# Later places in the queues for what follows the addition of a chunk's parts in the up projection (transformer layer, one Trainium2 core)

## The chip, the cores and the metric

The kernel runs on one core of one Trainium2 chip. The metric is the device time of one launch in microseconds (us): median of several runs.

## What is computed

One decoder layer for 256 tokens of width 2048: two kinds of attention, an output projection, and an MLP. Only the MLP matters here; in the reference it is

```python
h = _rmsnorm(x, norm_mlp_pre[layer])
u = jnp.square(jax.nn.relu(h @ w_up[layer]))
x = x + _rmsnorm(u @ w_down[layer], norm_mlp_post[layer])
```

`w_up` is 2048 x 8192 and `w_down` 8192 x 2048, all in float32.

## The kernel before

**Precision and units of work.** A float32 factor is split into a high and a low part (`split`, lines 303 to 307: ScalarE copies the source to `hi`, VectorE subtracts to get `lo`; `split_gain`, lines 309 to 312, does the same with a gain). A product is then three matmuls into one bank of PSUM, high by high, low by high, high by low; `three` issues such a group of three through `mm`, and every matmul of the MLP therefore has line 296. A transpose on TensorE is `transpose`, line 300.

**The up projection.** Its 8192 columns are done in eight chunks of 1024, numbered 0 to 7 (`for j in range(FF // CW)` in `layer`). A chunk has four accumulators of 128 tokens x 512 columns, one PSUM bank each: `PARTS` (0,0), (0,1), (1,0), (1,1), token block first, column half second. The steps of a chunk come from a table, `UP_STEPS`. A step `k` is one 128-row piece of the weights: four groups of three matmuls, one for each accumulator. A step `p` or `w` covers two pieces by a fast-multiplication scheme with seven products in place of eight (`seven_products`): its sums of weight blocks (`t`, `u`, made by VectorE from the raw blocks `ab`) are split like other weights, and four of its products go into four more banks, `m`. Chunks 1 to 5 have eight steps `k` and four of the other kind, chunks 6 and 7 ten and three. While chunk j runs, chunk j - 1's four banks are needed again for `m`, and their evacuation has to be over by then.

**Putting a chunk together.** The four `m` are combined after the last step of the seven-product kind (`close`, line 1072 on ScalarE, line 1075 on VectorE, result in tile `c`). At the end of the chunk's last step one generator `up_evac` is started for each accumulator. It adds the part from `c` to the accumulator in place (line 969, VectorE), applies Relu with the token's scale (line 973, ScalarE, tile `r`), transposes the four 128 x 128 blocks of `r` on TensorE back into the same bank (`rt`), and squares the bank into tile `uT` (line 991, ScalarE). `r` has two buffers. The tiles are numbered by column half: the halves of chunk 5 are `j` = 10 and 11 in `up_evac`, those of chunk 7 are 14 and 15. So `rt10_0` is chunk 5, first half, first token block.

**What sets the order.** Instructions are written in a fixed order, engine by engine. Besides the loop over matmuls there are generators; each yields the delay after which it wants to go on, and `Flow` keeps a model clock that only advances by the planned cost of TensorE's instructions (0.216 us for a matmul of 512 columns). After each group of three matmuls `flow.pump()` lets every generator whose time has come issue its next instructions. A delay therefore does not make any engine wait: it only decides behind which matmuls of the next chunk, and behind which splits of coming weights, an instruction stands in its engine's queue. In `up_evac` the delays are 0.2 us ahead of the addition, a fixed one behind it, then `UP_STEP` (2.2 us) times `order`, where `order` is 0.75 times the part's number 0 to 3, then the Relu, and `D_UP` (1.8 us) from there to the transposes, behind which the square follows directly. Since generators go on only after a group of three matmuls (0.65 us of the model clock), each delay is rounded up to whole groups.

Weights are split up to six tiles ahead of use into eight buffers `hi` and eight `lo`; a load into `raw` (five buffers, queue SP) or `ab` (queue POOL) is issued when its buffer is free.

After chunk 7 the down projection begins at once: its first matmuls (tile `y`) run while chunk 7 is put together, and its left factors are the `uT` tiles, split into `uhi` and `ulo`.

Of the kernel before, what the change touches and what calls it, by code (L numbers as in the profile page):

```python
# [263 lines left out]
def layer(nc, tc, io):  # L264
# [13 lines left out]
    def bank(i, name):  # L278
        return ps.tile([P, 512], F32, tag=f"bank{i}", bufs=1, name=name)
# [19 lines left out]
    def transpose(out, a):  # L299
        nc.tensor.transpose(out, a, ident)  # L300
        flow.spend(TR)
# [663 lines left out]
    def up_evac(j, b, i, acc, order, more=None):  # L965

        if more is not None:
            yield 0.2
            nc.vector.tensor_tensor(out=acc, in0=acc, in1=more, op=OP.add)
            yield 1.4  # L970
        yield UP_STEP * order
        r = late["up"].tile([P, 512], F32, tag="r", bufs=2, name=f"r{j}_{b}")
        nc.scalar.activation(r, acc, AF.Relu, scale=rstd2[b])
        yield D_UP if j > 1 else 2 * D_UP
        t = bank(i, f"rt{j}_{b}")
        for k in range(4):
            transpose(t[:, k * P:(k + 1) * P], r[:, k * P:(k + 1) * P])
        if j not in uT:
            if j in (12, 13):
                t2 = late["ab"][:, (j - 12) * CW:(j - 11) * CW]  # L980
            elif j in (8, 9):
                if j == 8:
                    late["uT8"] = late["up"].tile([P, 2 * CW], F32, tag="uT8", bufs=1, name="uT8")
                t2 = late["uT8"][:, (j - 8) * CW:(j - 7) * CW]
            elif j == 10:
                t2 = late["up"].tile([P, CW], F32, tag="uT10", bufs=1, name="uT10")
            else:
                tag = {"tag": "T", "bufs": 2} if j > 13 else {}
                t2 = late["up"].tile([P, CW], F32, name=f"uT{j}", **tag)
            uT[j] = t2.rearrange("p (k s) -> p k s", k=4)  # L990
        nc.scalar.activation(uT[j][:, :, b * P:(b + 1) * P], t.rearrange("p (k s) -> p k s", k=4), AF.Square)
# [91 lines left out]
    for j in range(FF // CW):  # L1083
# [9 lines left out]
        for t, b in order:  # L1093
# [18 lines left out]
            if what == "k":  # L1112
                w = weights.get(tiles[0])
                h_done(k, b)
                for n in range(2):
                    c = slice(n * 512, (n + 1) * 512)
                    three(accs[b, n], [tok(hT[x], k, b) for x in range(2)], [w[x][:, 0, c] for x in range(2)], t == 0, t == len(steps) - 1)
                    if t == len(steps) - 1:
                        evac.append(flow.start(up_evac(2 * j + n, b, at[b, n], accs[b, n], 0.75 * (2 * b + n),
                                                       more[b, n] if j else None)))  # L1120
                    flow.pump()
                if b == NB - 1:
                    weights.free(tiles[0])
                continue
# [208 lines left out]
```

## Time and profile before

| | |
|---|---|
| device time, median of 3 runs | 1051.41 us (1051.28 to 1051.68) |
| the profiled execution: its own time | 1050.67 us |
| the profiled execution: span from first to last instruction | 1048.9 us |
| TensorE matmul busy | 1036.4 us, 99% of the span |
| VectorE busy | 810.6 us, 77% |
| ScalarE busy | 633.0 us, 60% |
| mean granted TensorE clock | 0.998 |

The first line of the table is what a result is compared with. The profile is of one execution, whose span leaves out 1.77 us of its own time; positions below are microseconds from the span's start. PE is TensorE, PEld its weight loads, DVE VectorE, ACT ScalarE, POOL GpSimd and SP the queue that issues most loads. A row of the timeline has start, duration, engine, line, operation and tiles; in brackets stand the idle time of the engine before it and what ended that. Ends of matmuls are modelled, so starts are what is compared. The up projection's chunks 2 to 7 begin at about 444, 487, 530, 573, 616 and 660 us, and the down projection at 704 us.

### The profile page before, as it was taken

Reading aid. Unit: us, or ns where it says so; the run is one execution under the profiler, and the core shown is the slowest. Engines: PE = TensorE matmul, PEld = TensorE weight load, DVE = VectorE, ACT = ScalarE, POOL = GpSimd, SP = SyncE. Lnnn points to the kernel's source line nnn. Section 1 sums busy time; section 2 is a strip of 40 time slices with the busy share of each in tenths; the row PEclk is TensorE's granted clock in tenths of the full one; section 3 lists DMA queues with packets and bytes.
Section 4 is the critical chain, followed back from the end, with each engine's and each line's share of the span. In section 5 each row is a group of like instructions: output and inputs, shape, how many; then the busy total and the mean of one; then the engine's idle time right before and its main releaser. Section 6 shows DMA issues by size and latency. Waiting matters only on the chain.

```text
span 1048.9 us, 13584 instructions
## 1 busy us (share of the span) xinstructions
PE 1036.4 (99%) x4844; PEld 863.1 (82%) x4844; DVE 810.6 (77%) x1083; ACT 633.0 (60%) x846; POOL 98.9 (9%) x156
## 2 busy tenths in 40 slices
PE   9999999999999999999999999999999999999996
PEld 7888899888888788888888888888888888888885
DVE  6776546567557669988889798887899988989995
ACT  6675436565545466666756766656567564766661
POOL 0011111112111000010100000000000001112100
PEclk9999999999999999999999999999999999999999
DMA  9999879699878295766766656469778767788952
GB/s 298 369 298 298 221 197 321 197 258 300 227 219 259 84 362 180 281 207 241 262 214 222 228 191 212 139 227 322 249 272 312 267 226 260 264 301 318 368 196 81
DMA packets 93572, 260.81 MB, mean 249 GB/s; under 512 B 8768, under 2 KB 13376, under 8 KB 92096
## 3 DMA queue, kind: packets, MB, share of 16 engines
q1 hardware_dynamic: 71776, 190.61, 52.9%
q0 software_dynamic: 21152, 68.69, 23.0%
q8 instruction: 38, 0.62, 0.2%
q10 hardware_dynamic: 576, 0.64, 0.2%
q14 instruction: 30, 0.25, 0.1%
HBM read 244.18 MB, written 39.32 MB: 270 GB/s over the span
## 4 chain that ended last, share of the span: by engine, by line
PE 87%; DVE 6%; DMA 3%; issue 2%; ACT 2%; POOL 0%; DVEq 0%; POOLq 0%; SPq 0%; ACTq 0%
PE y L296 26%; PE acc_u L296 17%; PE acc_o L296 8%; PE m L296 6%; PE md L296 5%; PE acc_qk L296 4%; PE acc_v L296 4%; PE acc_cq L296 2%; PE acc_ukv L296 2%; PE acc_q L296 2%; PE acc_k L296 2%; DMA raw<-in_w_up 2%; DVE lo L307 2%; PE acc_uq L296 2%; PE acc_ckv L296 1%
## 5 line engine op out<-in xcount | busy, mean ns | idle before, releaser
L307 DVE TENSOR_TENSOR lo<-raw,hi 128x1024 fp32r<-128x1024 f32 (+3 forms) x241 | 269.7, 1137 | 96.3 <-ACT hi L306 95.5
L306 ACT ACTIVATE hi<-raw 128x1024 fp32r<-128x1024 f32 (+3 forms) x241 | 234.7, 988 | 98.0 <-PE y L296 21.5
L296 PE MATMUL y<-hi,uhi 128*128 128x512 f32 x376 | 146.7, 390 | 0.0
L296 PE MATMUL y<-hi,ulo 128*128 128x512 f32 x376 | 146.3, 389 | 0.0
L296 PE MATMUL y<-lo,uhi 128*128 128x512 f32 x376 | 146.3, 389 | 0.0
L296 PE MATMUL acc_u<-hi,hT_hi 128*128 128x512 f32 x356 | 141.7, 398 | 0.0
L296 PE MATMUL acc_u<-hi,hT_lo 128*128 128x512 f32 x356 | 139.2, 391 | 0.4 <-DVE hT_lo L307 0.4
L296 PE MATMUL acc_u<-lo,hT_hi 128*128 128x512 f32 x356 | 138.8, 390 | 0.0
L311 DVE SCALAR_TENSOR_TENSOR lo<-raw,gcol,hi 128x1024 fp32r<-128x1024 f32 x72 | 90.6, 1280 | 16.2 <-ACT hi L310 15.8
L310 ACT ACTIVATE hi<-raw,gcol 128x1024 fp32r<-128x1024 f32 x72 | 81.6, 1149 | 20.3 <-DMA raw<-in_w_up 12.8
L296 PEld LDWEIGHTS y<-hi,ulo 128*128 128x128 f32 x376 | 70.6, 188 | 14.8
L296 PEld LDWEIGHTS y<-hi,uhi 128*128 128x128 f32 x376 | 70.6, 188 | 14.6
L296 PEld LDWEIGHTS y<-lo,uhi 128*128 128x128 f32 x376 | 70.6, 188 | 14.4
L296 PEld LDWEIGHTS acc_u<-hi,hT_lo 128*128 128x128 f32 x356 | 66.8, 188 | 15.0 <-DVE hT_lo L307 0.8
L296 PEld LDWEIGHTS acc_u<-lo,hT_hi 128*128 128x128 f32 x356 | 67.0, 188 | 12.9
L296 PEld LDWEIGHTS acc_u<-hi,hT_hi 128*128 128x128 f32 x356 | 66.9, 188 | 12.9
L296 PE MATMUL m<-hi,st 128*128 128x512 f32 x156 | 56.5, 389 | 0.0
L296 PE MATMUL acc_o<-hi,mixT_hi 128*128 128x512 f32 x128 | 51.8, 405 | 0.0
L307 DVE TENSOR_TENSOR lo<-st_down,hi 128x1024 fp32r<-128x1024 f32 x40 | 48.0, 1220 | 3.9 <-ACT hi L306 3.8
L296 PE MATMUL acc_o<-hi,mixT_lo 128*128 128x512 f32 x128 | 50.2, 392 | 0.0
L296 PE MATMUL acc_o<-lo,mixT_hi 128*128 128x512 f32 x128 | 50.0, 390 | 0.0
L306 ACT ACTIVATE hi<-st_down 128x1024 fp32r<-128x1024 f32 x40 | 42.1, 1052 | 10.8 <-PE y L296 9.4
(331 smaller groups left out, 2037.6 us busy)
## 6 DMA issues: line engine op xcount, KB each, us to landing
raw<-in_w_down SPq DMA_DIRECT2D x88, 512.0 KB, 5.8
raw<-in_w_up SPq DMA_DIRECT2D x86, 512.0 KB, 4.6
raw<-in_w_in SPq DMA_DIRECT2D x55, 512.0 KB, 6.5
raw<-in_w_out SPq DMA_DIRECT2D x32, 512.0 KB, 7.3
ab<-in_w_up POOLq DMA_DIRECT2D x28, 512.0 KB, 5.1
sums<-in_w_up SPq DMA_DIRECT2D x20, 512.0 KB, 7.9
ab_down<-in_w_down POOLq DMA_DIRECT2D x20, 512.0 KB, 6.3
tu<-sums POOLq DMA_DIRECT2D x8, 1024.0 KB, 5.1
```

The source lines that it names most:

```text
L296: nc.tensor.matmul(out, a, b, start=start, stop=stop)
L306: nc.scalar.activation(hi, src, AF.Copy)
L307: nc.vector.tensor_tensor(out=lo, in0=src, in1=hi.bitcast(F32), op=OP.subtract)
L310: nc.scalar.activation(hi, src, AF.Copy, scale=g)
L311: nc.vector.scalar_tensor_tensor(out=lo, in0=src, scalar=g, in1=hi.bitcast(F32), op0=OP.mult, op1=OP.subtract)
```

## The change

One line: the delay that `up_evac` yields after the addition, where there is one (chunks 1 to 7). It was 1.4 us for all; now it is 1.8 us for column halves 2 to 9 (chunks 1 to 4) and 2.4 us for halves 10 to 15 (chunks 5, 6 and 7).

```diff
@@ -967,7 +967,7 @@
         if more is not None:
             yield 0.2
             nc.vector.tensor_tensor(out=acc, in0=acc, in1=more, op=OP.add)
-            yield 1.4
+            yield 1.8 if j < 10 else 2.4
         yield UP_STEP * order
         r = late["up"].tile([P, 512], F32, tag="r", bufs=2, name=f"r{j}_{b}")
         nc.scalar.activation(r, acc, AF.Relu, scale=rstd2[b])
```

No instruction is added or removed. On TensorE, the four transposes of each part of chunk 5 stand one group of three matmuls further on, here the first part's, in the second step of chunk 6 (`acc_u6` are chunk 6's accumulators, `hi258` and `lo258` a weight tile, `hT` the left factor):

```order
-L300 MATMUL rt10_0_5631<-ident_94,r10_0_5620 128x128 x4
 L296 MATMUL acc_u6_00_5608<-hi258_5527,hT_hi_2925 128x512
 L296 MATMUL acc_u6_00_5608<-lo258_5528,hT_hi_2925 128x512
 L296 MATMUL acc_u6_00_5608<-hi258_5527,hT_lo_2926 128x512
+L300 MATMUL rt10_0_5640<-ident_94,r10_0_5623 128x128 x4
```

The same holds for all four parts of chunks 5, 6 and 7; in chunks 1 to 4 only the last part, (1,1), moves, by one group as well, and nothing else does on any engine.

On ScalarE, at the same place (`r` Relu, `uT` square, `hi264` the split of a sum of weights that stands ahead of need):

```order
-L973 ACTIVATE r10_0_5620<-acc_u5_00_5233,rstd_pre20_3418 128x512
-L991 ACTIVATE uT10_5636<-rt10_0_5631 128x4x128
-L973 ACTIVATE r11_0_5638<-acc_u5_01_5234,rstd_pre20_3418 128x512
-L306 ACTIVATE hi264_5642<-u6_0_5550 128x1024
-L991 ACTIVATE uT11_5660<-rt11_0_5655 128x4x128
-L973 ACTIVATE r10_1_5662<-acc_u5_10_5235,rstd_pre21_3513 128x512
+L973 ACTIVATE r10_0_5623<-acc_u5_00_5233,rstd_pre20_3418 128x512
+L306 ACTIVATE hi264_5633<-u6_0_5550 128x1024
+L991 ACTIVATE uT10_5645<-rt10_0_5640 128x4x128
+L973 ACTIVATE r11_0_5647<-acc_u5_01_5234,rstd_pre20_3418 128x512
+L991 ACTIVATE uT11_5663<-rt11_0_5658 128x4x128
+L973 ACTIVATE r10_1_5665<-acc_u5_10_5235,rstd_pre21_3513 128x512
```

The first Relu keeps its place; the split `hi264` now stands ahead of the first square and the second Relu, not behind them. Chunk 6's parts in chunk 7 move in the same way.

On ScalarE at the start of the down projection, where chunk 7 is put together (`uhi0_1` and `hi308` are splits of a left factor and of a weight tile):

```order
-L973 ACTIVATE r14_0_6359<-acc_u7_00_5971,rstd_pre20_3418 128x512
-L991 ACTIVATE uT14_6375<-rt14_0_6370 128x4x128
-L973 ACTIVATE r15_0_6377<-acc_u7_01_5972,rstd_pre20_3418 128x512
-L306 ACTIVATE uhi0_1_6379<-uT1_3816 128x1024
-L306 ACTIVATE hi308_6385<-raw308_6383 128x1024
+L973 ACTIVATE r14_0_6362<-acc_u7_00_5971,rstd_pre20_3418 128x512
+L306 ACTIVATE uhi0_1_6370<-uT1_3816 128x1024
+L306 ACTIVATE hi308_6376<-raw308_6374 128x1024
+L991 ACTIVATE uT14_6388<-rt14_0_6383 128x4x128
+L973 ACTIVATE r15_0_6390<-acc_u7_01_5972,rstd_pre20_3418 128x512
```

Here two splits pass the first square and the second Relu. On VectorE the splits' second halves (`lo264` and its like) keep their places; POOL's queue is the same, and so is SP's.

## The prediction

> **What bounds the kernel now.** I read the page's first lines, then the view of waits for TensorE, then the timeline at each place where the change moves something.
>
> ```profile
> span 1048.9 us, 13584 instructions
> PE 1036.4 (99%) x4844; PEld 863.1 (82%) x4844; DVE 810.6 (77%) x1083; ACT 633.0 (60%) x846; POOL 98.9 (9%) x156
> ...
> PE rt L300 <- ACT r L973: 1.2, 3, 0.5
> ```
>
> TensorE is busy 1036.4 of 1048.9 us. Only 12.5 us are left, head and tail of the program among them, so what a new order can gain is small, and what it can lose is whatever new wait it gives TensorE. The third line is what the change can touch: the transposes of a chunk's Relu tile waited for that Relu three times, 1.2 us in all, at most 0.5 us at a time. The timeline shows where. First TensorE where chunk 5 is put together; the second piece is the next transposes there, which wait for nothing:
>
> ```profile
> 618.07 0.39 PE L296 MATMUL acc_u<-hi,hT_lo 128*128 128x512 f32 x1
> 618.98 0.65 PE L300 MATMUL rt<-ident,r 128*128 128x128 f32 x4 [0.52 <-ACT r L973]
> 619.39 0.49 PE L296 MATMUL acc_u<-hi,hT_hi 128*128 128x512 f32 x1
> 619.72 0.40 PE L296 MATMUL acc_u<-lo,hT_hi 128*128 128x512 f32 x1
> ...
> 621.34 0.40 PE L296 MATMUL acc_u<-hi,hT_lo 128*128 128x512 f32 x1
> 621.58 0.60 PE L300 MATMUL rt<-ident,r 128*128 128x128 f32 x4
> 621.93 0.48 PE L296 MATMUL acc_u<-hi,hT_hi 128*128 128x512 f32 x1
> 622.24 0.39 PE L296 MATMUL acc_u<-lo,hT_hi 128*128 128x512 f32 x1
> ```
>
> From the last matmul ahead of the transposes to the second one behind them pass 619.72 - 618.07 = 1.65 us with the wait and 622.24 - 621.34 = 0.90 us without. The stall costs 0.75 us, more than the 0.52 that the bracket counts, because the modelled ends of matmuls hide some of it and the restart is a little slower. The same where chunk 6 is put together, and the remaining places: chunk 1 (first line) and chunk 7 (last three lines).
>
> ```profile
> 447.39 0.66 PE L300 MATMUL rt<-ident,r 128*128 128x128 f32 x4 [0.17 <-ACT r L973]
> ...
> 662.21 0.39 PE L296 MATMUL acc_u<-hi,hT_lo 128*128 128x512 f32 x1
> 663.12 0.66 PE L300 MATMUL rt<-ident,r 128*128 128x128 f32 x4 [0.52 <-ACT r L973]
> ...
> 663.84 0.39 PE L296 MATMUL acc_u<-lo,hT_hi 128*128 128x512 f32 x1
> ...
> 706.33 0.39 PE L296 MATMUL y<-hi,ulo 128*128 128x512 f32 x1
> 706.56 0.60 PE L300 MATMUL rt<-ident,r 128*128 128x128 f32 x4
> 709.08 0.38 PE L300 MATMUL rt<-ident,r 128*128 128x128 f32 x2
> ```
>
> For chunk 6 the stall is 663.84 - 662.21 - 0.90 = 0.73 us. Chunk 7's transposes begin 0.23 us after the matmul ahead of them, the ordinary step: no wait there. Chunk 1's wait of 0.17 us is at its first part, which the change doesn't move.
>
> **The change, part by part.** *The first transposes of chunks 5 and 6* go behind one more group of three matmuls. One group lasts 0.68 us on TensorE (first line, from the chain); the other lines are the Relu that is waited for at 618.98 with the addition ahead of it, and the Relu at 663.12.
>
> ```profile
> 632.00 0.68 PE m L296 x3
> ...
> 617.51 1.89 DVE L969 TENSOR_TENSOR acc_u<-acc_u,c 128x512 f32<-128x512 f32 x3
> ...
> 618.24 0.69 ACT L973 ACTIVATE r<-acc_u,rstd_pre 128x512 f32<-128x512 f32 x1 [4.12 <-DVE acc_u L969]
> ...
> 662.38 0.69 ACT L973 ACTIVATE r<-acc_u,rstd_pre 128x512 f32<-128x512 f32 x1 [4.12 <-DVE acc_u L969]
> ```
>
> ScalarE had been idle 4.12 us before this Relu: it starts when VectorE's addition ends, wherever it is queued, and its place behind `hi263` is the old one. So it still ends at 618.24 + 0.69 = 618.93. TensorE, without waiting, would now come to the transposes at 618.07 + 0.23 + 0.68 = 618.98, the very time at which they began with the wait, 0.05 after the Relu's end. For chunk 6: Relu over at 663.07, TensorE there at 662.21 + 0.23 + 0.68 = 663.12, where they began too. The wait is filled with a group of useful matmuls and nothing is left of it, but with no margin.
>
> The gain at each place is therefore at least the group that is now done ahead, 0.68 us, and at most the whole stall, 0.75 and 0.73. Two places give 1.36 to 1.48 us. The difference is the slower restart, 0.05 to 0.07 a time, which stays if `r` comes only just in time. I take 1.4, nearer the lower end, since 0.05 us is no lead.
>
> [...]
>
> *Whether the second gain adds to the first* depends on VectorE. If VectorE's additions for chunk 6 came at a fixed time, TensorE, 0.7 us ahead, would wait again. These rows follow what sets VectorE's pace between the two places.
>
> ```profile
> 632.04 1.06 ACT L306 ACTIVATE hi<-ab 128x1024 fp32r<-128x1024 f32 x1 [2.09 <-PE acc_u L296]
> ...
> 633.13 1.23 DVE L307 TENSOR_TENSOR lo<-ab,hi 128x1024 fp32r<-128x1024 f32 x1 [1.96 <-ACT hi L306]
> ...
> 634.65 0.54 POOL L377 DMA_DIRECT2D ab<-in_w_up  x1 [2.65 <-DVE lo L307]
> ...
> 639.21 1.23 DVE L359 TENSOR_TENSOR t<-ab 128x1024 f32<-128x1024 f32 x1 [2.58 <-DMA ab<-in_w_up]
> ...
> DVE lo L307 <- ACT hi L306: 0.2, 1, 0.2
> ```
>
> Read upwards from the fourth: VectorE waited 2.58 us for a load, which POOL issued when VectorE had read the buffer, which waited for ScalarE's split, which had waited 2.09 us for TensorE to free a weight buffer. So this chain starts at TensorE and comes 0.7 us earlier when TensorE does. From there to chunk 6's additions VectorE works nearly without a break: the last line is all of its waits from 640 to 659. The gains add.
>
> *The splits that now pass a square and a Relu* on ScalarE (`hi264`, `hi286`, `uhi0_1` and `hi308`) delay these two. The tightest place is chunk 7, with two splits:
>
> ```profile
> 705.38 0.69 ACT L973 ACTIVATE r<-acc_u,rstd_pre 128x512 f32<-128x512 f32 x1 [0.28 <-DVE acc_u L969]
> 707.20 0.60 ACT L991 ACTIVATE uT<-rt 128x512 f32<-128x512 f32 x1 [1.12 <-PE rt L300]
> 707.69 0.68 ACT L973 ACTIVATE r<-acc_u,rstd_pre 128x512 f32<-128x512 f32 x1
> 708.26 1.06 ACT L306 ACTIVATE uhi<-uT 128x1024 fp32r<-128x1024 f32 x1
> 709.21 1.06 ACT L306 ACTIVATE hi<-raw 128x1024 fp32r<-128x1024 f32 x1
> ```
>
> In these positions the new order is: Relu 705.38, `uhi0_1` 0.57 later at 705.95, `hi308` 0.95 later at 706.90, the square 0.95 after that at 707.85, the second Relu 0.49 later, over at 708.34 + 0.68 = 709.02. The second transposes come to their turn 0.68 us later than 709.08, at 709.76. That leaves 0.7 us. At chunks 5 and 6 one split passes, and the sum is alike: 618.24 + 0.57 + 0.95 + 0.49 + 0.68 = 620.93 against 621.58. The cost is nothing as long as the passing splits don't wait themselves. `hi308` needs the buffer of the down projection's first weight tile, whose last matmul starts at 706.33 and ends 0.39 later, 706.72, ahead of 706.90; and it needs its load, issued by SP at 698.45 and 6.4 us on its way, so there at 704.85:
>
> ```profile
> 698.45 0.33 SPq L188 DMA_DIRECT2D raw<-in_w_down  x1
> ...
> raw<-in_w_down SPq DMA_DIRECT2D x1, 512.0 KB, 6.4
> ```
>
> *Chunks 1 to 4, part (1,1), and the squares behind it* come one group later. What stands behind the square on ScalarE is a split, and behind that one which waits for TensorE anyway:
>
> ```profile
> 498.36 0.60 ACT L991 ACTIVATE uT<-rt 128x512 f32<-128x512 f32 x1 [0.83 <-PE rt L300]
> 498.86 1.05 ACT L306 ACTIVATE hi<-ab 128x1024 fp32r<-128x1024 f32 x1
> 500.42 1.07 ACT L306 ACTIVATE hi<-u 128x1024 fp32r<-128x1024 f32 x1 [0.51 <-PE acc_u L296]
> ```
>
> Of 0.68 us the wait of 0.51 takes most; 0.17 is left, on splits that are made up to six tiles ahead. I count nothing, with or without a bound below: no transposes waited at chunks 2 to 4, so nothing can be won there either. The place in the queue of (1,1)'s last square against the reuse of its bank isn't close: chunk 6's `m` products begin at 632.00, the last transposes of chunk 5 at about 618.98 + 3 x 2.60 = 626.8 (2.60 is the step from the first to the second).
>
> *The down projection* starts 1.4 us earlier and must keep that. In its first stretch ScalarE waits for TensorE, not the other way round; TensorE has no wait behind 663.12.
>
> ```profile
> ACT hi L306 <- PE y L296: 17.5, 16, 2.1
> ```
>
> *Sum.* 0.7 + 0.7 + 0 + 0 = 1.4 us. Against the profiled execution's own time, 1050.67 (span 1048.9 and 1.77 around it), that is 1049.3. The median of the runs is 0.74 above the profiled execution, so 1051.41 - 1.4 = **1050.0 us**, 0.13% less. A measurement of this kernel can tell about 0.2% from no change, 2.1 us, so this counts as the same.
>
> **The rivals.** *Only one stall goes.* If VectorE doesn't follow TensorE between the two places, TensorE comes to chunk 6's transposes 0.7 us early and waits it away: gain 0.7, time 1050.7. Against it speaks the chain above; for it, that neither place has any margin: 0.05 us.
>
> *The change doesn't do what it says.* If the Relu is over as much later as the transposes are queued, the same wait stays and the time is 1051.4. It would take a later addition or a split ahead of the Relu; the order shows neither.
>
> *A wait in place of the one removed, and slower.* `hi308` now stands ahead of the first square and second Relu of chunk 7. If it starts at L, the second transposes can start at L + 0.95 + 0.49 + 0.68 + 0.05 = L + 2.17; TensorE wants them at 709.76. So it decides from L = 707.6, that is, when the load takes 9.1 us and not 6.4. Landing times of such loads there (first line) and of tile `ab`'s anywhere (second line), least, median and most:
>
> ```profile
> DMA to landing us min/median/max: 5.3/6.5/8.9
> ...
> DMA to landing us min/median/max: 3.7/5.1/12.1
> ```
>
> With the slowest of all, 12.1, L is 710.55, TensorE stalls 2.96 us and the kernel ends 1.6 us slower than before, at 1053.0. To lose 2.1 us the load would have to take 12.7. With the slowest seen here, 8.9, nothing is lost. [...]
>
> **How the numbers follow.** Forecast, both stalls gone: 0.80. Only one: 0.09. No effect: 0.04. The load's wait: 0.03. What I don't see, either way: 0.04. The forecast's own range is 1.36 to 1.48 off the fastest and slowest run of before, 1051.28 and 1051.68: 1049.8 to 1050.3. I widen it below by 0.3 for what the restart might give besides, and above to take in the one-stall case with the runs' spread, 1051.0: 1049.5 to 1051.0. Faster by over 0.2% would need more than both stalls are worth: 0.02, half of the unseen. Slower by over 0.2%: a third of the load's case and the other half of the unseen: 0.03. The same: 0.95.
>
> **What would show it.** In the changed kernel's profile the waits of transposes for the Relu should be one of 0.17 us, at chunk 1, and at chunks 5 and 6 0.1 us or less; chunk 5's first transposes should still begin at about 618.98, with one more group done, and chunk 6's at 663.12 - 0.68 = 662.4; chunk 7's, which come one group later but 1.4 us earlier, at 706.56 + 0.68 - 1.4 = 705.8. It is wrong if a wait of 0.2 us or more stands at a first or second transposes of chunks 5 to 7, or if TensorE waits anywhere in the down projection.

## The result, and the profile after

| | before | after |
|---|---|---|
| median of 22 runs each | 1051.00 us (1050.08 to 1052.77) | 1049.78 us (1048.81 to 1050.90) |
| ratio, 95% interval | | 0.9986 (0.9980 to 0.9992) |
| profiled execution, span | 1048.9 us | 1047.3 us |

By the ratio the change makes the kernel 0.14% faster, 1.5 us of 1051.0 with an interval from 0.8 to 2.1; the medians differ by 1.22 us. With 22 runs on each side that is told apart from nothing. It lies inside the bound of 0.2% that the prediction took for one measurement.

TensorE's waits in the changed kernel, the whole view (who waited for whom; us in total, times, longest):

```profile
PE warm L537 <- DVE zero L534: 1.2, 1, 1.2
PE acc_u L296 <- DVE hT_lo L307: 0.4, 1, 0.4
PE rt L300 <- ACT r L973: 0.4, 1, 0.4
PE qrt L300 <- DVE qT L804: 0.2, 1, 0.2
```

Of the three waits of transposes for a Relu one is left, and it is chunk 1's, at 447.03. At chunks 5 and 6 TensorE's timeline now reads:

```profile
618.46 0.39 PE L296 MATMUL acc_u<-hi,hT_lo 128*128 128x512 f32 x1
618.69 0.66 PE L300 MATMUL rt<-ident,r 128*128 128x128 f32 x4
619.10 0.48 PE L296 MATMUL acc_u<-hi,hT_hi 128*128 128x512 f32 x1
...
661.92 0.39 PE L296 MATMUL acc_u<-hi,hT_lo 128*128 128x512 f32 x1
662.15 0.66 PE L300 MATMUL rt<-ident,r 128*128 128x128 f32 x4
662.57 0.48 PE L296 MATMUL acc_u<-hi,hT_hi 128*128 128x512 f32 x1
```

The transposes start the ordinary 0.23 us behind the matmul ahead of them, and no wait stands in brackets. What stayed is the slower restart: 619.10 - 618.69 = 0.41 us from the transposes to the next matmul, as in the stalled rows of before, not 0.35. The weight loads of TensorE differ along with it. Here are the loads of the first transposes in the changed kernel, and of the second ones in the kernel before, which had their Relu early:

```profile
618.68 0.42 PEld L300 LDWEIGHTS rt<-ident,r 128*128 128x128 f32 x4 [0.26 <-ACT r L973]
...
621.34 0.59 PEld L300 LDWEIGHTS rt<-ident,r 128*128 128x128 f32 x4
```

With `r` early the load starts 0.24 us ahead of the transposes at 621.58, beside the matmul that started at 621.34; with `r` just in time it starts 0.01 us ahead of those at 618.69. All 24 transposes of chunks 5 to 7 in these two profiles go this way: where the load starts 0.22 to 0.24 us ahead, the step to the next matmul is 0.35 or 0.36 us (20 of them), and where it starts 0 to 0.01 us ahead, 0.41 or 0.42 (the first ones of chunks 5 and 6, in both). ScalarE at chunk 5 shows why there was no margin:

```profile
617.94 0.69 ACT L973 ACTIVATE r<-acc_u,rstd_pre 128x512 f32<-128x512 f32 x1 [4.11 <-DVE acc_u L969]
618.53 1.05 ACT L306 ACTIVATE hi<-u 128x1024 fp32r<-128x1024 f32 x1
619.48 0.58 ACT L991 ACTIVATE uT<-rt 128x512 f32<-128x512 f32 x1
619.96 0.69 ACT L973 ACTIVATE r<-acc_u,rstd_pre 128x512 f32<-128x512 f32 x1
```

The Relu ends at 618.63, 0.06 us ahead of the transposes. The split now stands between it and the first square; the second Relu is over at 620.65, and its transposes come at 621.27. Chunk 7, first ScalarE, then its first and second transposes on TensorE:

```profile
703.75 0.69 ACT L973 ACTIVATE r<-acc_u,rstd_pre 128x512 f32<-128x512 f32 x1 [0.29 <-DVE acc_u L969]
704.34 1.05 ACT L306 ACTIVATE uhi<-uT 128x1024 fp32r<-128x1024 f32 x1
705.28 1.05 ACT L306 ACTIVATE hi<-raw 128x1024 fp32r<-128x1024 f32 x1
706.23 0.60 ACT L991 ACTIVATE uT<-rt 128x512 f32<-128x512 f32 x1
706.73 0.68 ACT L973 ACTIVATE r<-acc_u,rstd_pre 128x512 f32<-128x512 f32 x1
...
705.60 0.60 PE L300 MATMUL rt<-ident,r 128*128 128x128 f32 x4
708.12 0.60 PE L300 MATMUL rt<-ident,r 128*128 128x128 f32 x4
```

Both splits run without a wait, and the second Relu is over at 707.41, 0.7 us ahead of its transposes.

**A better yardstick than the span.** Where spans differ, part of the difference lies far ahead of chunks 5 and 6. The time from chunk 4's first transposes to the last matmul leaves that out (and with it part (1,1) of chunks 1 to 3, which the change moves too). Before and after:

```profile
575.58 0.38 PE L300 MATMUL rt<-ident,r 128*128 128x128 f32 x2
...
1040.06 0.39 PE L1210 MATMUL y<-hi,ulo 128*128 128x512 f32 x1
```

```profile
575.28 0.38 PE L300 MATMUL rt<-ident,r 128*128 128x128 f32 x2
...
1038.42 0.39 PE L1210 MATMUL y<-hi,ulo 128*128 128x512 f32 x1
```

(The last matmuls are issued at line 1210 and not at line 296.) 1040.06 - 575.58 = 464.48 us before, 1038.42 - 575.28 = 463.14 after: 1.34 us gained. I call it the stretch below.

### The profile page after: what moved, and what is told of

Same layout as the page of the kernel before. It is cut to its first block, busy times and chain, and to the rows that moved or that the text cites. A ratio compares the mean times of both kernels' runs of the same rounds, so it can differ in the third digit from the quotient of the medians.

```text
span 1047.3 us, 13583 instructions
## 1 busy us (share of the span) xinstructions
PE 1036.7 (99%) x4844; PEld 863.6 (82%) x4844; DVE 809.9 (77%) x1083; ACT 632.4 (60%) x846; POOL 98.7 (9%) x156
## 4 chain that ended last, share of the span: by engine, by line
PE 96%; DVE 2%; issue 1%; ACT 0%; POOL 0%; DVEq 0%; POOLq 0%; ACTq 0%
PE y L296 26%; PE acc_u L296 23%; PE acc_o L296 8%; PE m L296 7%; PE md L296 5%; PE acc_qk L296 4%; PE acc_v L296 4%; PE acc_ckv L296 2%; PE acc_ukv L296 2%; PE acc_q L296 2%; PE acc_cq L296 2%; PE acc_k L296 2%; PE acc_uq L296 2%; PE rt L300 1%; PE sc_b L296 1%
```

## The experiments

Theory: TensorE's two waits for a Relu are filled with a group of matmuls, and that is all. Main rival: ScalarE's new order, in which splits of weights stand ahead of squares, makes weights ready earlier. The ratios are to the kernel before with their 95% intervals; each set of runs is some ten executions of the kernel, against about thirty of the kernel before on the same chip (the first four kernels on one chip, the others on a second). The intervals reach about 1 us to either side, so half a microsecond can't be told by them, and the stretch and the rows, of one profile each, carry the verdicts.

| kernel | ratio | stretch, us | against 464.48 |
|---|---|---|---|
| chunks 5 and 6 alone | 0.9989 (0.9980 to 0.9998) | 463.11 | -1.37 |
| the rest without 5 and 6 | 1.0002 (0.9993 to 1.0011) | 464.47 | -0.01 |
| one group earlier | 1.0018 (1.0009 to 1.0028) | 466.15 | +1.67 |
| two groups later | 0.9991 (0.9982 to 1.0000) | 463.06 | -1.42 |
| chunk 5 alone | 0.9998 (0.9989 to 1.0007) | 463.85 | -0.63 |
| squares late, TensorE as before | 1.0002 (0.9993 to 1.0010) | 464.46 | -0.02 |
| chunk 7 three groups later | 0.9988 (0.9980 to 0.9997) | 463.14 | -1.34 |
| chunk 1 two groups later too | 0.9977 (0.9968 to 0.9986) | 463.14 | -1.34 |
| chunk 1 alone | 0.9996 (0.9987 to 1.0004) | 464.45 | -0.03 |
| two groups at 1, 5 and 6 | 0.9977 (0.9968 to 0.9986) | 463.04 | -1.44 |
| the change again | 0.9988 (0.9980 to 0.9997) | 463.14 | -1.34 |

**Which part of the change.** First the two halves of it.

```diff
-            yield 1.4
+            yield 2.4 if 10 <= j < 14 else 1.4
```

> The delay is 2.4 us for chunks 5 and 6 alone; chunk 7 and chunks 1 to 4 keep 1.4 us. Theory (a group of matmuls fills TensorE's two waits for the Relu): all of the gain, 1.36 us off the kernel before, 0.13%; no wait of transposes at chunks 5 and 6. Rival (the gain comes from splits that ScalarE and VectorE now make earlier, at all moved places): part of the gain, 0.5 to 1 us.

```diff
-            yield 1.4
+            yield 1.8 if j < 10 else 2.4 if j > 13 else 1.4
```

> The other half: 1.8 us for chunks 1 to 4, 2.4 us for chunk 7, and 1.4 us as before for chunks 5 and 6. Theory: no gain, 0 us, both waits of 0.52 us still in the profile. Rival (earlier splits): 0.3 to 0.9 us faster, since chunk 7 is where two splits pass.

Chunks 5 and 6 carry all of the gain, 1.37 us of the stretch, and the rest carries none, 0.01 us. The rest keeps the waits; TensorE at chunk 6 there:

```profile
662.17 0.39 PE L296 MATMUL acc_u<-hi,hT_lo 128*128 128x512 f32 x1
663.08 0.66 PE L300 MATMUL rt<-ident,r 128*128 128x128 f32 x4 [0.52 <-ACT r L973]
```

Moving what had no wait at chunk 7 and in part (1,1) of chunk 4 bought nothing and cost nothing. Part (1,1) of chunks 1 to 3 lies ahead of the stretch: from chunk 1's first transposes to chunk 4's pass 128.23 us here and 128.19 before, so nothing was won there either.

**More and less of it.**

```diff
-            yield 1.4
+            yield 0.7 if j > 9 else 1.4
```

> The delay is 0.7 us for chunks 5, 6 and 7, which puts what follows one group of matmuls earlier than in the kernel before, and 1.4 us for chunks 1 to 4. Theory: each wait grows by the group that is no longer ahead, 0.68 us at chunks 5 and 6, and chunk 7, whose Relu was over at 706.07 for transposes at 706.56, gets a wait of about 0.3: 1.7 us slower than before, waits of 1.2, 1.2 and 0.2 us by the profile's count. Rival (earlier splits): ScalarE's splits come later here, about as much slower as the change was faster, 1.4 us, but with no larger waits for the Relu.

The stretch is 1.67 us longer, the forecast was 1.7. TensorE at chunks 5, 6 and 7:

```profile
618.29 0.65 PE L300 MATMUL rt<-ident,r 128*128 128x128 f32 x4 [1.20 <-ACT r L973]
...
663.11 0.66 PE L300 MATMUL rt<-ident,r 128*128 128x128 f32 x4 [1.20 <-ACT r L973]
...
706.32 0.39 PE L296 MATMUL y<-hi,ulo 128*128 128x512 f32 x1
706.80 0.44 PE L300 MATMUL rt<-ident,r 128*128 128x128 f32 x2
```

Each wait has grown from 0.52 to 1.20, by the 0.68 us of one group. Chunk 7 now loses too: 0.48 us from matmul to transposes in place of 0.23, a gap of 0.25 that the view of waits doesn't list since the modelled ends cover it (the forecast had 0.2 in that view). The rival expected no larger waits for the Relu; it fails here.

```diff
-            yield 1.4
+            yield 1.8 if j < 10 else 3.0
```

> The delay is 3.0 us for chunks 5, 6 and 7: one group of matmuls later than in the changed kernel. Theory: the Relu is now 0.7 us ahead of its transposes, so the slower restart goes too: 0.05 to 0.07 us at each of two places, 1.48 us off the kernel before, 0.1 better than the change, which timing can hardly tell; the profile must show the step from transposes to the next matmul as 0.35 us and not 0.41. Rival (earlier splits): about another 0.5 us faster, since one more split passes at chunks 5 and 6. Rival (a split that now stands ahead makes the second transposes wait): slower than the change, with a new wait there.

TensorE at chunk 6 in this kernel:

```profile
664.12 0.39 PE L296 MATMUL acc_u<-hi,hT_lo 128*128 128x512 f32 x1
664.35 0.60 PE L300 MATMUL rt<-ident,r 128*128 128x128 f32 x4
664.70 0.48 PE L296 MATMUL acc_u<-hi,hT_hi 128*128 128x512 f32 x1
```

With the transposes one more group behind their Relu the step is 0.35 us, not 0.41, as forecast, and the stretch is 0.08 us shorter than the change's. No 0.5 us came from the further split that passes, and no new wait either. The timing can't tell it from the change.

**Do the two gains add?**

```diff
-            yield 1.4
+            yield 2.4 if 10 <= j < 12 else 1.4
```

> The delay is 2.4 us for chunk 5 alone, 1.4 us for all others. Theory (the two gains add, since VectorE follows TensorE between the two places): half the gain, 0.68 us off the kernel before, and chunk 6's wait still 0.52 us by the profile's count, with its Relu 0.7 us earlier in step with TensorE. Rival (VectorE keeps its own time, so a gain at chunk 5 is waited away at chunk 6): no gain at the end, and a wait of 1.2 us at chunk 6.

The ratio alone is inconclusive: its interval holds both 0 and 0.68 us. The stretch is 0.63 us shorter. At chunk 6, which this kernel leaves as it was, the wait is that of before and not 1.2:

```profile
662.68 0.66 PE L300 MATMUL rt<-ident,r 128*128 128x128 f32 x4 [0.56 <-ACT r L973]
```

So VectorE and ScalarE did follow TensorE between the two places, but for 0.04 us, and the gains add.

**ScalarE's order alone.**

```diff
+        if j > 9:
+            yield 0.6
         nc.scalar.activation(uT[j][:, :, b * P:(b + 1) * P], t.rearrange("p (k s) -> p k s", k=4), AF.Square)
```

> The kernel before, with a further delay of 0.6 us between the transposes and the square of chunks 5 to 7: TensorE's order is that of the kernel before, while on ScalarE splits and Relus pass the squares as in the change. Theory: no gain, 0 us, and both waits of 0.52 us stay. Rival (the gain comes from ScalarE's order): the change's gain, 1.4 us, with TensorE's order untouched.

ScalarE and TensorE at chunk 5 in this kernel:

```profile
619.07 1.29 ACT L973 ACTIVATE r<-acc_u,rstd_pre 128x512 f32<-128x512 f32 x2 [4.12 <-DVE acc_u L969]
620.25 1.05 ACT L306 ACTIVATE hi<-u 128x1024 fp32r<-128x1024 f32 x1
621.20 0.59 ACT L993 ACTIVATE uT<-rt 128x512 f32<-128x512 f32 x1
...
619.81 0.44 PE L300 MATMUL rt<-ident,r 128*128 128x128 f32 x2 [0.52 <-ACT r L973]
```

The split stands ahead of the square, as in the change, and starts 0.44 us behind the transposes' start, where it was 1.76 in the kernel before (620.74 against 618.98). The wait and the time are the old ones. The order is not quite the change's: here the second Relu passes the square too and still stands ahead of the split. Together with the kernel in which only chunk 7's splits pass, and with the waits that grew by a whole group, the rival is out: the gain is in TensorE's order.

**A split that waits, ahead of a Relu.**

```diff
-            yield 1.8 if j < 10 else 2.4
+            yield 1.8 if j < 10 else 2.4 if j < 14 else 3.7
```

> The changed kernel, with a delay of 3.7 us for chunk 7: two groups of matmuls later than in the change, three than before. On ScalarE the splits hi309 and hi310, which wait for TensorE to free a weight buffer, now stand ahead of a square and a Relu. Theory: chunk 7 had no wait to fill, so the time is the change's, 1.4 us off the kernel before, as long as the Relus are over in time. Rival (a split that waits holds the Relu behind it, and TensorE waits for that): a new wait at chunk 7's second to fourth transposes of 0.5 us or more, and slower than the change by that.

The stretch is the change's to 0.01 us, and there is no wait of transposes in this profile. ScalarE there:

```profile
710.80 0.68 ACT L973 ACTIVATE r<-acc_u,rstd_pre 128x512 f32<-128x512 f32 x1
711.70 1.06 ACT L306 ACTIVATE hi<-raw 128x1024 fp32r<-128x1024 f32 x1 [0.22 <-PE y L296]
712.82 0.60 ACT L991 ACTIVATE uT<-rt 128x512 f32<-128x512 f32 x1
713.32 0.68 ACT L973 ACTIVATE r<-acc_u,rstd_pre 128x512 f32<-128x512 f32 x1
...
712.19 0.60 PE L300 MATMUL rt<-ident,r 128*128 128x128 f32 x4
714.71 0.60 PE L300 MATMUL rt<-ident,r 128*128 128x128 f32 x4
```

`hi309`, at 708.86, didn't wait. `hi310` does wait for TensorE, 0.22 us, but it holds nothing up: the square behind it starts 0.63 us after its transposes at 712.19, and where no split waits ahead of a square that step is 0.64 as well (709.67 to 710.31 in this profile). The Relu behind it is over at 714.00, 0.7 us ahead of its transposes at 714.71. So this kernel didn't put the rival to the test. That such a split could hold TensorE up if it waited longer isn't refuted; with a late load it wasn't tried here.

**Chunk 1, which the change leaves out.** Its wait differed from profile to profile, up to 1.17 us, twice that of chunks 5 and 6.

```diff
-            yield 1.8 if j < 10 else 2.4
+            yield 3.0 if j < 4 else 1.8 if j < 10 else 2.4
```

> The changed kernel, with a delay of 3.0 us for chunk 1 also: all four parts of chunk 1 two groups later than in the kernel before. Chunk 1's wait for the Relu was 0.17, 0.37, 0.71, 1.06, 0.17 and 1.17 us in the six profiles so far. Theory: two groups, 1.36 us, cover it, so on average 0.6 us by the profile's count and about 0.2 of hidden time and slower restart go too: 0.8 us better than the change, 2.2 off the kernel before; no wait of transposes is left. Rival (chunk 1's wait comes from a late load which TensorE then meets elsewhere): no better than the change, with the wait at another place.

```diff
-            yield 1.4
+            yield 3.0 if j < 4 else 1.4
```

> The kernel before with a delay of 3.0 us for chunk 1 alone. Theory: chunk 1's wait goes, 0.4 to 0.9 us off the kernel before, and both waits of 0.52 us at chunks 5 and 6 stay; from chunk 4's first transposes to the last matmul the time is that of the kernel before, 464.5 us. Rival (TensorE, come earlier out of chunk 1, meets the late load's effect again): no gain, a new wait in chunk 2 or 3.

```diff
-            yield 1.4
+            yield 3.0 if j < 4 or 10 <= j < 14 else 1.4
```

> A delay of 3.0 us for chunks 1, 5 and 6 and 1.4 us for the others. Theory: all three waits go and the slower restart too: 1.48 + 0.8, 2.3 us off the kernel before, 0.1 better than with one group at chunks 5 and 6; from chunk 4's first transposes to the last matmul 463.0 us; no transposes wait. Rival (two groups later is too late for something): slower than the change.

TensorE at chunks 1, 5 and 6 in the last of these:

```profile
447.39 0.60 PE L300 MATMUL rt<-ident,r 128*128 128x128 f32 x4
447.74 0.48 PE L296 MATMUL acc_u<-hi,hT_hi 128*128 128x512 f32 x1
...
618.25 0.60 PE L300 MATMUL rt<-ident,r 128*128 128x128 f32 x4
618.60 0.48 PE L296 MATMUL acc_u<-hi,hT_hi 128*128 128x512 f32 x1
...
661.65 0.60 PE L300 MATMUL rt<-ident,r 128*128 128x128 f32 x4
662.00 0.48 PE L296 MATMUL acc_u<-hi,hT_hi 128*128 128x512 f32 x1
```

No wait and no slow restart is left. From chunk 0's first transposes to chunk 2's pass 86.10, 86.09 and 86.12 us in these three kernels; in the ten profiles in which chunk 1's first part stands where it was, 86.28 to 87.46, 86.83 on average. That is 0.73 us less, and the later chunks keep it: no new wait stands in chunks 2 and 3. Two of the three are the fastest kernels here, both 0.23% off the kernel before. Against the change, timed beside the last of them, the medians are 1048.49 and 1049.71 us. Chunk 1 alone was too small for the timing to show (interval 0.9987 to 1.0004); its stretch is that of before, as it should be.

The change itself was timed once more with these:

> The changed kernel once more, on the chip of the next two, so that they can be compared with it. Theory: 1.4 us off the kernel before, chunk 1's wait anywhere between 0.2 and 1.2 us.

Its ratio was 0.9988, and chunk 1's wait 0.40 us.

## Why the prediction was right

*The two waits are filled and nothing is left of them:* right. Forecast 1.36 to 1.48 us, 1.4 taken; the stretch gave 1.34, under the lower end by no more than profiles of like kernels differ (0.03), and the timing 1.5 us by the ratio, which can't tell these apart. That the absolute time came so close, 1049.78 for 1050.0, is partly luck: it was reckoned from 1051.41, the median of three runs, and 22 runs put the kernel before at 1051.00.

*The slower restart stays when the Relu is only just ready:* right, and it decides between the two ends. In the changed kernel the step is 0.41 us at chunk 5's first transposes, with the Relu 0.06 us ahead, and 0.35 at the second (621.27 to 621.62), with it 0.62 ahead; a second group brought 0.08 of the expected 0.1 us. The load starts 0.01 us ahead of the transposes in the one case and 0.23 in the other (621.04). The lower end, two groups of 0.68 us with the slower restart kept, is 1.36; measured 1.34.

*The first Relu keeps its time:* right, it ends 0.06 us ahead of its transposes, forecast 0.05. The absolute position 618.98 came out as 618.69, because this execution was 0.30 us earlier already at chunk 4 (575.28 against 575.58).

*The second gain adds to the first:* right, shown by chunk 5 alone. The changed kernel shows the chain too: chunk 6's first Relu starts at 661.41 against 662.38, 0.97 us earlier, that is 0.67 beyond the 0.30 at chunk 4. That it followed so closely took some luck, since a load stands in the chain: its wait was 2.68 us in place of 2.58, and a later wait of 0.20 that was no longer there made up for it.

*The passing splits, chunk 7, part (1,1) of chunks 1 to 4 cost nothing:* right; the kernel without chunks 5 and 6 has the stretch of before to 0.01 us, and the margin at chunk 7 was the 0.7 us worked out. The splits that pass at chunks 5 and 6 brought TensorE no wait: the last one in the changed kernel is chunk 1's, at 447.03. Nor has TensorE a wait at chunk 7 in any profile in which `hi308` passes, so what a late load of it would have cost stays an estimate.

*The down projection keeps what it gets:* right, no wait of TensorE stands behind chunk 1's.

*Where the reasoning was thin:* chunk 1's wait was taken from one profile as 0.17 us and left aside. It is 0 to 1.17 us, so it was no constant of the kernel, only a sample. It didn't touch this forecast, as the change doesn't move it.

## What to carry to other kernels

TensorE was busy for 99% of the span here, and its instructions stand in a fixed order. A Relu that came 0.68 us late (0.91 us from start to start against 0.23) cost the kernel 0.67 us at each of two places, 1.34 in the stretch, and one group of 0.68 us moved ahead of its consumer took that away. Some lead takes the slow restart too: with 0.06 us of it the step was still 0.41 us, and with 0.49, at chunk 7 before, 0.35 (706.56 to 706.91). So size how late a result is, and move its consumer behind independent work worth at least that. Only consumers that wait are worth moving: the rest of the change gave 0.01 us. Before sizing such a wait, look at it in several profiles: chunks 5 and 6 repeated theirs, chunk 1, whose producer hung on a load shortly before in seven of nine profiles, did not (0 to 1.17 us), and there the margin should cover the worst of several.

## What the runs showed of the hardware that was not expected

Chunk 1's wait follows one split on ScalarE, held by a load in seven of the nine profiles, the change's repeat aside, in which chunk 1's first part stands where it was. Here is the latest case, from the kernel two groups later, with VectorE and the Relu in between:

```profile
440.15 1.15 ACT L310 ACTIVATE hi<-raw,gcol 128x1024 fp32r<-128x1024 f32 x1 [3.35 <-DMA raw<-in_w_up]
...
441.33 1.28 DVE L311 SCALAR_TENSOR_TENSOR lo<-raw,gcol,hi 128x1024 fp32r<-128x1024 f32 x1 [1.58 <-ACT hi L310]
...
447.91 0.69 ACT L973 ACTIVATE r<-acc_u,rstd_pre 128x512 f32<-128x512 f32 x1 [3.72 <-DVE acc_u L969]
...
447.10 0.39 PE L296 MATMUL acc_u<-hi,hT_lo 128*128 128x512 f32 x1
448.65 0.55 PE L300 MATMUL rt<-ident,r 128*128 128x128 f32 x3 [1.17 <-ACT r L973]
```

The split starts 6.95 us ahead of TensorE's last matmul before the transposes, and the wait is 1.17; the sum is 8.12. In the kernel before it is 446.83 - 438.87 + 0.17 = 8.13, in one group earlier 446.15 - 438.19 + 0.17 = 8.13, in the rest without 5 and 6 445.87 - 438.81 + 1.06 = 8.12. In all nine the transposes begin 8.50 to 8.52 us after that split starts. The way from one to the other leads over VectorE: ScalarE was idle for 3.72 us ahead of the Relu and waited for the addition, while VectorE, once the split's second half had come, worked up to that addition without a break in this profile. So where a load holds the split, the time at which it lands passes to TensorE's transposes unchanged in these profiles.

From chunk 4's first transposes to the last matmul, profiles of kernels with the same waits agree to 0.03 us (463.11 to 463.14 in five of them), while the position at which that stretch begins goes from 574.90 to 576.86 in the ten that leave chunk 1's first part where it was. What differs from one execution to the next in these profiles lies ahead of chunk 4.

A wait's bracket understated its cost: 0.52 us in brackets were 0.75 on TensorE, since ends of matmuls are modelled (start to start the gap was 0.91 against 0.23, 0.68 more) and 0.06 us of restart come after.
